# A hybrid decoder layer on one core: the operand tiles of the up and down projections are moved to other bytes of SBUF

## The chip, the cores and the metric

The kernel runs on one core of one Trainium2 chip. The metric is the device time of one execution in microseconds (us). A profile of one execution lies beside the times; its span runs from the first to the last instruction of the program, and it is a little shorter than the execution's own time.

In what follows a *byte* of a tile is its address inside one SBUF partition: all 128 partitions hold a tile at the same byte. A matmul instruction has two SBUF operands. The *stationary* one (128 x 128) is loaded into the array by a weight load ahead of it; the *moving* one (128 rows of N columns) streams through. One moving *row* here means the N contiguous float32 values that one matmul reads in each partition, so a row of 256 is 1024 bytes.

## The reference

One layer of a hybrid decoder: an RMS norm, a combined input projection, differential attention beside a gated linear recurrence (HGRN2), an output projection with a residual, and a feed-forward part with a causal convolution of width 3. The change lies in the feed-forward part:

```python
D_MODEL = 1024; SEQ = 1024; D_FF = 2816; CONV_WIDTH = 3
def conv_ffn(a, w_up, conv_w, conv_b, w_down):
    u = a @ w_up
    u = lax.conv_general_dilated(u, conv_w[:, None, :], ...) + conv_b
    gate, up = jnp.split(u, 2, axis=-1)
    return (jax.nn.gelu(gate, approximate=True) * up) @ w_down
...
    a = rmsnorm(h, ln_ffn_pre[l])
    y = conv_ffn(a, w_ffn_up[l], ffn_conv_w[l], ffn_conv_b[l], w_ffn_down[l])
    h = h + rmsnorm(y, ln_ffn_post[l])
```

## The kernel before

**Precision.** Every float32 matrix product is made of three matmuls: each operand is split into a rounded high part and the rest (`split`, lines 146 to 151; `t_split`, lines 1222 to 1226), and high x high, high x low and low x high are summed in PSUM. The low parts are made by VectorE or GpSimd, the high parts by ScalarE.

**The up stage** multiplies the 1024 model columns by the 2 x 2816 columns of `w_up`. The sequence is worked on in two pieces, p = 0 and p = 1, and each product is a Strassen-like scheme of seven products, j = 0 to 6, on quarters of the operands. The moving operands are the split tiles `tt[p][j]`: four rows of high parts, then four rows of low parts, each row `WN[p]` long, 258 for p = 0 and 256 for p = 1. `t_tiles` (1215) allocates them; `t_split` fills them; `t_sums` (1233) makes those of j = 1, 2, 3, 5 from sums of quarters. The stationary operands are the split weights `uh`, `ul`, made two products ahead by `prep` (1107).

The first feature tile is done by `plain_unit` (1316) with eight plain products instead of seven; `t_sums` of both pieces run beside it. The other 21 feature tiles go through `unit` (1335), which both pieces step through in turn (loop at 1453): product j of p = 0, product j of p = 1, then j + 1. `mm` (1341) is one such product: twelve matmuls, called a *block* here:

```python
for k in range(4):
    s = slice(P * k, P * (k + 1))
    T.matmul(pt, hi[:, s], th[:, k], ...)   # line 1346
    T.matmul(pt, hi[:, s], tl[:, k], ...)   # line 1347
    T.matmul(pt, lo[:, s], th[:, k], ...)   # line 1348
```

TensorE's order is written out by hand (`manual_schedule`), so its instructions run in program order. Products 0 and 4 add into the PSUM tile `pa`, 1, 3 and 5 into `pb`, 2 and 6 into `pc`. Behind the last product of a feature tile `gated` (1309) does the convolution (`conv`, 1300), the gate and the store of the result to `gsc` in DRAM.

**The down stage** multiplies the gated tiles, read back from DRAM, by `w_down`, again in seven products (`ORDER`, 1403) of eleven steps each. `operands` (1423) loads and splits both sides of a step three steps ahead (`LOOK`). Here the gated tile `gh`, `gl` is the stationary side (four slices of 128 columns) and the weight tile `wh`, `wl` is the moving side, 512 columns. One step is twelve matmuls (`mms`, 1499, lines 1504 to 1506), 77 steps in all.

**The out stage** ahead of the up stage (`out_part`, 997, lines 1002, 1004, 1006) also has moving rows of 512, `wo`, against stationary slices of the tiles `mp`. The change doesn't touch it, but the prediction reads some of its rows.

**Where the tiles lie.** Pools are stacked from both ends of a partition: those on the left grow upward, those on the right downward, and in a pool the tags follow one another in the order in which they are first asked for. This is the allocation of the program before, with the remainder by 512, of the rows that the matmuls read:

| tile | role | pool | base byte | base mod 512 | row pitch |
|---|---|---|---|---|---|
| t0_6, t0_5 | moving, N = 258 | mix (`X1`, `X2`) | 5856, 14112 | 224, 288 | 1032 |
| t1_6 | moving, N = 256 | mix (`X0`) | 22368 | 352 | 1032 |
| t1_0, t1_4, t1_5 | moving, N = 256 | tsplit | 51424, 59616, 67808 | 224 | 1024 |
| t0_1, t0_2, t0_3 | moving, N = 258 | tsplit | 76000, 84256, 92512 | 224, 288, 352 | 1032 |
| t1_1, t1_2, t1_3 | moving, N = 256 | tsplit2 | 100768, 108960, 117152 | 416 | 1024 |
| t0_4, t0_0 | moving, N = 258 | early | 163680, 171936 | 352, 416 | 1032 |
| uh, ul | stationary, up | weights, sums | several | 480 | 512 (slice) |
| gh, gl | stationary, down | down | 136896 and on | 192 | 512 (slice) |
| wh, wl | moving, N = 512, down | weights | 212960 and on | 480 | one row |

t0_7 and t1_7, which only `plain_unit` reads, lie where t0_5 and t1_5 lie later. Of the out stage, the first two steps read moving rows at byte class 480 (mod 512) with stationary slices of the first block at class 224 and of the second at class 288.

Of the kernel before, what the change touches and what calls it, by code (L numbers as in the profile page):

```python
# [9 lines left out]
F32 = mybir.dt.float32  # L10
F32R = mybir.dt.float32r
# [6 lines left out]
P = 128  # L18
# [13 lines left out]
WN = [258, 256]  # L32
# [53 lines left out]
def layer_kernel(ctx: ExitStack, tc: tile.TileContext, x, meta, table, lbl, gpre, gpost, win,  # L86
# [7 lines left out]
    def pool(name, bufs, side="left", space=None):  # L94
        kw = {"side": side} if space is None else {"space": space}
        cm = tc.tile_pool(name=name, bufs=bufs, reuse_waits="tile", **kw)
        return cm, cm.__enter__()

    def close(*cms):
        for cm in cms:  # L100
            cm.__exit__(None, None, None)
# [63 lines left out]
    mx_cm, mxp = pool("mix", 1)  # L165
# [1046 lines left out]

    tt = [[None] * 8 for _ in range(2)]

    def t_tiles(p, j, where, tag):
        if len(tag) == 1:
            both = where.tile([P, 8, WN[p]], F32R, tag=tag[0], name=f"t{p}_{j}")
            return both[:, 0:4], both[:, 4:8]
        both = where.tile([P, 8, int(tag[1])], F32R, tag=tag[0], name=f"t{p}_{j}")
        return both[:, 0:4, : WN[p]], both[:, 4:8, : WN[p]]  # L1220

    def t_split(p, j, src, where, *tag):
        hi, lo = t_tiles(p, j, where, tag)
        A.copy(hi, src)
        V.tensor_tensor(lo, src, hi.bitcast(F32), op=ALU.subtract)
        tt[p][j] = (hi, lo)

    def quarter(p, j):
        n = WN[p]
        a, c = {0: (0, 0), 7: (0, n), 4: (4, 0), 6: (4, n)}[j]  # L1230
        return at2[p][:, a:a + 4, c:c + n]

    def t_sums(p, where, last):
        b11, b12, b21, b22 = (quarter(p, j) for j in (0, 7, 4, 6))
        V.tensor_tensor(b11, b12, b11, op=ALU.subtract)
        V.tensor_tensor(b12, b22, b12, op=ALU.subtract)
        V.tensor_tensor(b22, b22, b11, op=ALU.subtract)
        t_split(p, 1, b22, where, f"t{p}_1")
        t_split(p, 2, b11, where, f"t{p}_2")
        t_split(p, 3, b12, where, f"t{p}_3")  # L1240
        V.tensor_tensor(b21, b21, b22, op=ALU.subtract)
        t_split(p, 5, b21, *last)

# [47 lines left out]

    xu_cm, xup = pool("xu", 2)
    t_cm, tp = pool("tsplit", 1)

    marks = {}

# [85 lines left out]
        next(p0)  # L1382
    trans(8)
    t_split(1, 7, quarter(1, 7), tp, "t1_5")
    t_split(1, 6, quarter(1, 6), mxp, "X0", WN[0])
    t_sums(0, tp, (mxp, "X2", WN[0]))
    close(a_cms.pop())
    t2_cm, t2p = pool("tsplit2", 1)
    p1 = plain_unit(1, ps_b)
    for j in range(4):  # L1390
        prep(7 + j)
        next(p1)
    t_sums(1, t2p, (tp, "t1_5"))
    close(a_cms.pop(), b_cm)
    v_cm, cv = pool("conv", 2, "right")
    dn_cm, dn = pool("down", 4, "right")
    next(p0)
    for j in range(4, 7):
# [257 lines left out]
```

## Time and profile before

| | us |
|---|---|
| median of 3 runs (lowest, highest) | 1313.61 (1312.26, 1313.94) |
| the profiled execution's own time | 1313.97 |
| its span | 1312.2 |
| up stage, first to last matmul of lines 1346 to 1348 | 663.5 to 1085.3, 3528 matmuls |
| down stage, first to last matmul of lines 1504 to 1506 | 1085.4 to 1302.7, 924 matmuls |

The mean granted clock of TensorE was 0.996 over the span.

How to read it. PE is TensorE's matmul side and PEld its weight loads, which overlap the matmuls; DVE is VectorE, ACT ScalarE, POOL GpSimd. A matmul row of the timeline has its start, its duration and its form ("128x256" is a moving operand of 256 columns). Matmuls are pipelined: a row lasts some 0.28 us, but the next one starts much earlier, so the time that a matmul costs is the step from its start to the start of the next. The program's names stand without their numbers (`t` for t1_2, `uh` for a split weight), so a block is told by its place: each feature tile runs the fourteen blocks (j, p) = (0,0), (0,1), (1,0), (1,1), ... (6,1) in this order.

### The profile page before, as it was taken

To read this page: it belongs to the slowest core of one execution; us is meant where nothing else is said; L and a number is where in the kernel's file an instruction comes from. 1 tells how busy PE (TensorE), PEld (TensorE's weight loads), DVE (VectorE), ACT (ScalarE), POOL (GpSimd) and SP (SyncE) were. 2 spreads that over 40 slices of the span, in tenths; PEclk is the share of its full clock that TensorE was granted. 3 is DMA by queue.
4 is the path that set the end of the run, shared out by engine and by line. 5 is a ranking of instruction groups with operands and counts; after the bars stand their busy time and mean duration, and the time that the engine had idled before them with its cause. 6 is when DMAs were issued, how large, how long until landed. Compare 5 with 4: busy or idle time off the path is not lost.

```text
span 1312.2 us, 26128 instructions
## 1 busy us (share of the span) xinstructions
PE 1283.2 (98%) x10172; PEld 1184.9 (90%) x10172; DVE 884.6 (67%) x1487; ACT 694.8 (53%) x1635; POOL 484.7 (37%) x384
## 2 busy tenths in 40 slices
PE   8999999999999999899999999999999999999997
PEld 7899999999999998677999999999999997888875
DVE  6564646465645574548897877778778767697586
ACT  8475466546644765247754544544544445464453
POOL 5231423242323310335066576666666631010121
PEclk9999999999999999999999999999999999999999
DMA  6244655173644534586322222222222138865263
GB/s 211 93 94 92 118 120 114 54 143 84 120 122 79 121 109 143 173 267 236 130 65 82 89 73 81 77 86 81 73 76 95 57 102 275 314 200 161 88 209 121
DMA packets 116322, 165.00 MB, mean 126 GB/s; under 512 B 10035, under 2 KB 57427, under 8 KB 116198
## 3 DMA queue, kind: packets, MB, share of 16 engines
q1 hardware_dynamic: 92966, 151.79, 35.6%
q0 software_dynamic: 23232, 11.54, 7.5%
q8 instruction: 80, 1.31, 0.4%
q14 instruction: 44, 0.36, 0.1%
HBM read 134.19 MB, written 52.17 MB: 142 GB/s over the span
## 4 chain that ended last, share of the span: by engine, by line
PE 83%; DVE 6%; ACT 4%; DMA 3%; issue 2%; POOL 2%; SPq 0%; DVEq 0%; ACTq 0%; POOLq 0%
PE pd L1505 5%; PE pd L1506 5%; PE pd L1504 5%; PE pb L1346 4%; PE pb L1347 4%; PE pb L1348 4%; PE pa L1346 3%; PE pa L1348 3%; PE pa L1347 3%; PE pc L1346 3%; PE pc L1347 3%; PE pc L1348 3%; PE pa L723 3%; PE pi_hf L232 1%; PE pi_dk L236 1%
## 5 line engine op out<-in xcount | busy, mean ns | idle before, releaser
L1346 PE MATMUL pb<-t,uh 128*128 128x258 f32 x504 | 142.3, 282 | 2.5 <-DVE u L53 2.5
L1347 PE MATMUL pb<-t,uh 128*128 128x258 f32 x504 | 141.7, 281 | 0.0
L1348 PE MATMUL pb<-t,ul 128*128 128x258 f32 x504 | 141.5, 281 | 0.0
L1505 PE MATMUL pd<-wl,gh 128*128 128x512 f32 x308 | 122.0, 396 | 1.2 <-DVE wl L53 1.1
L1504 PE MATMUL pd<-wh,gh 128*128 128x512 f32 x308 | 121.7, 395 | 0.0
L1506 PE MATMUL pd<-wh,gl 128*128 128x512 f32 x308 | 121.6, 395 | 0.0
L53 DVE SCALAR_TENSOR_TENSOR c<-uu,cwt,c 128x514 f32<-128x514 f32 (+1 forms) x88 | 97.2, 1105 | 19.6 <-ACT c L53 18.9
L53 POOL TENSOR_TENSOR c<-c,c 128x514 f32<-128x514 f32 (+1 forms) x44 | 63.6, 1445 | 122.7 <-ACT c L53 120.6
L1346 PEld LDWEIGHTS pb<-t,uh 128*128 128x128 f32 x504 | 95.4, 189 | 3.0 <-DVE u L53 2.9
L1347 PEld LDWEIGHTS pb<-t,uh 128*128 128x128 f32 x504 | 95.5, 189 | 0.0
L1346 PE MATMUL pa<-t,uh 128*128 128x258 f32 (+1 forms) x336 | 95.2, 283 | 0.0
L1348 PEld LDWEIGHTS pb<-t,ul 128*128 128x128 f32 x504 | 95.2, 189 | 0.0
L1348 PE MATMUL pa<-t,ul 128*128 128x258 f32 (+1 forms) x336 | 95.1, 283 | 0.0
L1347 PE MATMUL pa<-t,uh 128*128 128x258 f32 (+1 forms) x336 | 94.8, 282 | 0.0
L1346 PE MATMUL pc<-t,uh 128*128 128x258 f32 (+1 forms) x336 | 94.4, 281 | 0.0
L1347 PE MATMUL pc<-t,uh 128*128 128x258 f32 (+1 forms) x336 | 94.0, 280 | 0.0
L1348 PE MATMUL pc<-t,ul 128*128 128x258 f32 (+1 forms) x336 | 93.7, 279 | 0.0
L53 DVE SCALAR_TENSOR_TENSOR c<-ug,cwt,c 128x514 f32<-128x514 f32 (+1 forms) x88 | 88.3, 1004 | 1.4 <-ACT c L53 0.6
L53 POOL TENSOR_TENSOR ul<-ws,uh 128x512 fp32r<-128x512 f32 x42 | 60.7, 1444 | 35.4 <-ACT uh L53 35.4
L1505 PEld LDWEIGHTS pd<-wl,gh 128*128 128x128 f32 x308 | 57.7, 187 | 16.5 <-DVE wl L53 2.5
L53 ACT CAST uh<-ra 128x512 fp32r<-128x512 f32 x67 | 41.0, 617 | 59.6 <-PE pb L1347 41.0
L53 DVE TENSOR_TENSOR ul<-ra,uh 128x512 fp32r<-128x512 f32 x42 | 38.6, 920 | 48.1 <-ACT uh L53 48.1
(374 smaller groups left out, 4178.3 us busy)
## 6 DMA issues: line engine op xcount, KB each, us to landing
ra<-in_wup_dram SPq DMA_DIRECT2D x88, 256.0 KB, 2.7
mp<-msc SPq DMA_DIRECT2D x23, 512.0 KB, 5.2
tsc<-in_wdown_dram SPq DMA_DIRECT2D x44, 256.0 KB, 4.9
wi<-tsc SPq DMA_DIRECT2D x44, 256.0 KB, 3.1
gi<-gsc SPq DMA_DIRECT2D x33, 256.0 KB, 4.3
wi<-in_wdown_dram SPq DMA_DIRECT2D x33, 256.0 KB, 5.3
gsc<-c SPq DMA_DIRECT2D x22, 257.0 KB, 2.1
tsc<-in_wdown_dram POOLq DMA_DIRECT2D x22, 256.0 KB, 7.2
```

Source lines behind the costliest of these rows:

```text
L53: ins = call(*args, **kw)
L232: T.matmul(pt, hi[:, s], ahi[:, k, t0:t1], start=(k == 0), stop=False)
L236: T.matmul(pt, lo[:, s], ahi[:, k, t0:t1], start=False, stop=(k == KD - 1))
L723: T.matmul(po[:, :P], w_, vn[:, j], start=(j == 0), stop=(j == i))
L1346: T.matmul(pt, hi[:, s], th[:, k], start=(first and k == 0), stop=False, skip_group_check=True)
L1347: T.matmul(pt, hi[:, s], tl[:, k], start=False, stop=False, skip_group_check=True)
L1348: T.matmul(pt, lo[:, s], th[:, k], start=False, stop=(k == 3), skip_group_check=True)
L1504: T.matmul(py, gh[:, s], wh, start=(k == 0 and pr not in (3, 7)), stop=False, skip_group_check=True)
L1505: T.matmul(py, gh[:, s], wl, start=False, stop=False, skip_group_check=True)
L1506: T.matmul(py, gl[:, s], wh, start=False, stop=(k == NH - 1), skip_group_check=True)
```

## The change

Tiles get other bytes. `t_tiles` allocates flat tiles and cuts the eight rows out of them with a pitch and an offset that are given with the tag; the tiles t0_1, t0_2, t0_3 get a pitch of 288 values and t0_3 an offset of 6; t1_6 gets its own length 256 as pitch and an offset of 16 values. Two tiles that nothing reads or writes are allocated ahead of others: `gap` (48 values) as the first of the pool tsplit, `gap2` (56 values) as the first of the pool of the convolution, which lies above the pool of the down stage's operands. No instruction is added or removed, and no shape of an operand changes.

```diff
+    ROW = 288
+
     def t_tiles(p, j, where, tag):
-        if len(tag) == 1:
-            both = where.tile([P, 8, WN[p]], F32R, tag=tag[0], name=f"t{p}_{j}")
-            return both[:, 0:4], both[:, 4:8]
-        both = where.tile([P, 8, int(tag[1])], F32R, tag=tag[0], name=f"t{p}_{j}")
-        return both[:, 0:4, : WN[p]], both[:, 4:8, : WN[p]]
+        tag, w, off = (tag + (WN[p], 0)[len(tag) - 1:])[:3]
+        n = 8 * w if w > WN[p] else 8 * w + off
+        flat = where.tile([P, n], F32R, tag=tag, name=f"t{p}_{j}")
+        if w > WN[p]:
+            both = flat.rearrange("p (a c) -> p a c", a=8)[:, :, off:off + WN[p]]
+        else:
+            both = flat[:, off:].rearrange("p (a c) -> p a c", a=8)
+        return both[:, 0:4], both[:, 4:8]
...
-        t_split(p, 1, b22, where, f"t{p}_1")
-        t_split(p, 2, b11, where, f"t{p}_2")
-        t_split(p, 3, b12, where, f"t{p}_3")
+        for j, b in ((1, b22), (2, b11), (3, b12)):
+            t_split(p, j, b, where, f"t{p}_{j}", *(() if p else (ROW, 6 if j == 3 else 0)))
...
     t_cm, tp = pool("tsplit", 1)
+    tp.tile([P, 48], F32, tag="gap", name="gap")
...
-    t_split(1, 6, quarter(1, 6), mxp, "X0", WN[0])
+    t_split(1, 6, quarter(1, 6), mxp, "X0", WN[1], 16)
...
     v_cm, cv = pool("conv", 2, "right")
+    cv.tile([P, 56], F32, tag="gap2", name="gap2", bufs=1)
     dn_cm, dn = pool("down", 4, "right")
```

## The prediction

> **What bounds the kernel now.** I read the page first, then the stages by windows, then the timeline of TensorE, block by block.
>
> ```profile
> span 1312.2 us, 26128 instructions
> PE 1283.2 (98%) x10172; PEld 1184.9 (90%) x10172; DVE 884.6 (67%) x1487; ACT 694.8 (53%) x1635; POOL 484.7 (37%) x384
> PE 83%; DVE 6%; ACT 4%; DMA 3%; issue 2%; POOL 2%; SPq 0%; DVEq 0%; ACTq 0%; POOLq 0%
> L1346 PE MATMUL pb<-t,uh 128*128 128x258 f32 x504 | 142.3, 282 | 2.5 <-DVE u L53 2.5
> L1505 PE MATMUL pd<-wl,gh 128*128 128x512 f32 x308 | 122.0, 396 | 1.2 <-DVE wl L53 1.1
> ```
>
> TensorE carries 83% of the chain that ended last. The windows (us, then busy us of each engine, clock, DMA share, GB/s) show how full it is where the change works:
>
> ```profile
> 663.40:1085.50 422.10, 419.62 (x3532) 419.07 (x3531) 321.59 (x466) 205.01 (x363) 263.54 (x182) 1.00 0.25 83
> 1085.50:1312.20 226.70, 216.44 (x925) 172.61 (x923) 167.22 (x243) 109.45 (x219) 26.78 (x17) 0.99 0.58 194
> 663.40:703.60 40.20, 37.72 (x314) 37.17 (x313) 34.48 (x44) 20.77 (x37) 31.51 (x19) 1.00 0.24 80
> 703.60:743.80 40.20, 40.20 (x341) 40.20 (x341) 30.23 (x45) 19.54 (x36) 25.75 (x19) 1.00 0.24 79
> 1085.00:1125.00 40.00, 38.90 (x169) 31.05 (x168) 30.10 (x44) 20.95 (x36) 3.30 (x2) 1.00 0.87 299
> 1125.00:1205.00 80.00, 80.00 (x344) 64.22 (x343) 64.57 (x101) 39.13 (x75) 6.42 (x4) 1.00 0.63 206
> ```
>
> From 703.6 on TensorE is never idle in the up stage, at the full granted clock, and VectorE, the next engine, is at 30.23 of 40.20 (75%). In the down stage VectorE is at 64.57 of 80 (81%). So a nanosecond off each matmul is a nanosecond off the end, as long as VectorE keeps up. The three rows in which it doesn't (start, duration, and in brackets the idle time and who ended it):
>
> ```profile
> 673.28 0.39 PE L1346 MATMUL pb<-t,uh 128*128 128x258 f32 x1 [1.08 <-DVE u L53]
> 680.68 0.39 PE L1346 MATMUL pb<-t,uh 128*128 128x258 f32 x1 [1.40 <-DVE u L53]
> 1092.48 0.50 PE L1505 MATMUL pd<-wl,gh 128*128 128x512 f32 x1 [1.10 <-DVE wl L53]
> ```
>
> Now one feature tile, the first matmul of each block and of the tile after it. A block is twelve matmuls; the step between two rows is its time.
>
> ```profile
> 726.58 0.28 PE L1346 MATMUL pa<-t,uh 128*128 128x258 f32 x1
> ...
> 728.02 0.28 PE L1346 MATMUL pa<-t,uh 128*128 128x256 f32 x1
> ...
> 729.46 0.28 PE L1346 MATMUL pb<-t,uh 128*128 128x258 f32 x1
> ...
> 730.90 0.28 PE L1346 MATMUL pb<-t,uh 128*128 128x256 f32 x1
> ...
> 732.31 0.28 PE L1346 MATMUL pc<-t,uh 128*128 128x258 f32 x1
> ...
> 733.73 0.28 PE L1346 MATMUL pc<-t,uh 128*128 128x256 f32 x1
> ...
> 735.09 0.29 PE L1346 MATMUL pb<-t,uh 128*128 128x258 f32 x1
> ...
> 736.54 0.28 PE L1346 MATMUL pb<-t,uh 128*128 128x256 f32 x1
> ...
> 737.92 0.29 PE L1346 MATMUL pa<-t,uh 128*128 128x258 f32 x1
> ...
> 739.37 0.28 PE L1346 MATMUL pa<-t,uh 128*128 128x256 f32 x1
> ...
> 740.80 0.28 PE L1346 MATMUL pb<-t,uh 128*128 128x258 f32 x1
> ...
> 742.22 0.28 PE L1346 MATMUL pb<-t,uh 128*128 128x256 f32 x1
> ...
> 743.65 0.28 PE L1346 MATMUL pc<-t,uh 128*128 128x258 f32 x1
> ...
> 745.09 0.28 PE L1346 MATMUL pc<-t,uh 128*128 128x256 f32 x1
> ...
> 746.51 0.28 PE L1346 MATMUL pa<-t,uh 128*128 128x258 f32 x1
> ```
>
> The steps, with the base bytes mod 512 of the table of tiles:
>
> - N = 256: t1_0 1.44 (byte 224), t1_1 1.41 (416), t1_2 1.36 (416), t1_3 1.38 (416), t1_4 1.43 (224), t1_5 1.43 (224), t1_6 1.42 (352, pitch 1032). Sum 9.87 us.
> - N = 258: t0_0 1.44, t0_1 1.44, t0_2 1.42, t0_3 1.45, t0_4 1.45, t0_5 1.42, t0_6 1.44.
>
> All N = 256 blocks do the same work with the same kind of weights, yet they take from 1.36 (113.3 ns a matmul) to 1.44 (120 ns). The three at class 224 are the slow ones and the three at class 416 the fast ones. But t1_1 and t1_2 have the same class and differ by 0.05: the byte is not all of it, something of what ran before a block stays in its pace.
>
> **The change part by part.** Nothing is computed anew; only bytes move.
>
> *The gap in tsplit, the offset of t1_6.* 48 values are 192 bytes, so t1_0, t1_4, t1_5 go to 51616, 59808, 68000: class 416. The pool grows by 192 bytes and by 3 x (9216 - 8256) bytes for the longer pitch, so tsplit2 goes up by 3072 = 6 x 512 and t1_1 to t1_3 stay at class 416. t1_6 starts 64 bytes later with a pitch of 1024: 22432, class 416. All seven N = 256 blocks then read every row at class 416. Bounds: at best all run like t1_2, 7 x 1.36 = 9.52, 0.35 us less for each of 21 feature tiles, 7.4 us; at worst all stick at the pace of t1_0, 7 x 1.44 = 10.08, 4.4 us lost. The mean of the three that are there today is 1.383, which makes 9.68 and 4.0 us. Two of these three (t1_2, t1_3) are near 1.37; I take 1.37, since the blocks of p = 0 that run between lose some of their odd bytes too: 9.59, 0.28 x 21 = **5.9 us**.
>
> *The pitch of 288.* t0_1, t0_2, t0_3 go to 76192, 85408 and 94624 + 24 = 94648. Rows are 1152 bytes apart, so their classes are 416, 32, 160, 288 (t0_3: 440, 56, 184, 312), the same for high and low parts, where today each row begins 8 bytes further than the one before and the low ones 32 bytes off. No block of 258 columns with such rows is in the trace. Today the three take 1.44 + 1.42 + 1.45 = 4.31. From above, the pace of t1_2 for 258 columns, 12 x 258 x 0.1133 / 256 = 1.37 each, saves 0.20 x 21 = 4.2 us; from below, all at 1.45 loses 0.8 us. They become as regular as the p = 1 tiles at 416, whose mean of 1.383 is a little above the best, so I take 1.40: 0.11 x 21 = **2.3 us**.
>
> *The four p = 0 tiles left alone* and the 48 p = 0 matmuls of the first feature tile: nothing (plus or minus 0.01 us a block by what runs before them, 0.8 us for all). The p = 1 half of the first feature tile, 96 matmuls at t1_0's pace, gains at most 96 x 6.7 ns = 0.6 us, of which I take 0.2: VectorE makes the sums then. The first feature tile behind it waits twice for VectorE (1.08 and 1.40 us); what TensorE gains there, about 0.4 us, it waits longer: minus 0.4. ScalarE and VectorE write the moved tiles once, with as many elements. Up stage: 5.9 + 2.3 + 0.2 - 0.4 = **8.0 us**.
>
> *The second gap.* 56 values are 224 bytes; the down pool hangs below, so `gh` and `gl` go from class 192 to 480, the class of the moving `wh` and `wl`, which stay. A run of the down stage today, 114 matmuls apart:
>
> ```profile
> 1179.87 0.40 PE L1504 MATMUL pd<-wh,gh 128*128 128x512 f32 x1
> ...
> 1206.47 0.39 PE L1504 MATMUL pd<-wh,gh 128*128 128x512 f32 x1
> ```
>
> 26.60 / 114 = 233.3 ns. Other stationary bytes under the same moving class stand in the out stage, six matmuls from each row to the next, first with slices at class 224, then at class 288:
>
> ```profile
> 510.40 0.39 PE L1002 MATMUL py<-woh,mp 128*128 128x512 f32 x1
> ...
> 511.76 0.40 PE L1002 MATMUL py<-woh,mp 128*128 128x512 f32 x1
> ...
> 513.16 0.39 PE L1002 MATMUL py<-woh,mp 128*128 128x512 f32 x1
> ```
>
> 1.36 / 6 = 226.7 ns, then 1.40 / 6 = 233.3. The first six have stationary and moving rows 256 bytes apart in class, equal mod 256, as the down stage will have them. Best: 6.7 ns x 924 = 6.2 us. Worst: t1_0 too has both sides equal mod 256 (224 and 480) and runs at 120 / 113.3 of the best; a down stage slowed alike runs at 240, 6.2 us lost. I take three quarters of the good end, **4.6 us**, as the good row has the same shape, and six matmuls behind another stage are a short proof. The wait of 1.10 us at 1092 swallows 24 matmuls' gain, 0.2 us, inside that quarter.
>
> [...]
>
> Sum: 8.0 + 4.6 = 12.6 us off 1313.97, the profiled execution's own time (1.8 above its span), which is 0.4 above the median; off the median, 1313.6 - 12.6 = **1301.0**.
>
> **The rivals.**
>
> *The stationary byte does nothing; only the up stage gains*: 1313.6 - 8.0 = 1305.6. For it: runs of six are short. Against: 1.36 and 1.40 in a row.
>
> *Bytes are inert; the pace of a block comes from its place*, from which PSUM tile it adds to or what runs beside it. Then nothing moves: 1313.6. For it: t1_1 and t1_2 differ at one class. Against: t1_0, t1_4 and t1_5, in three places and two PSUM tiles, are all slow and all at 224. [...]
>
> *Equal classes collide.* In the down stage weight load and moving row walk through the same byte class at once, as in t1_0: 240 ns, 6.2 us lost. It ends above the time before once the up stage brings less than 6.2, say when the N = 258 rows gain nothing and the N = 256 blocks keep their mean of today's three less some entries, about 2 us: 1313.6 + 6.2 - 2 = 1317.8. For it: t1_0 has equal classes and the slowest pace. Against: the six at 226.7.
>
> *VectorE becomes the bound.* Up: 30.23 per 40.20; 2% faster blocks make it 77%. It can't take the gain except where it already does.
>
> **How the numbers follow.** Forecast (both stages gain, in whatever shares) 0.50; up alone 0.26; nothing 0.09; collision 0.15. A measurement of this kernel can't tell less than 0.2% (2.6 us) from no change. Up alone is faster. Of the collision, a third still ends faster or level by the up stage. Faster 0.79, same 0.09, slower 0.12. Range: the best of all terms is 7.4 + 4.2 + 0.6 + 6.2 = 18.4, 1295.2, and 0.8 for the tiles left alone makes 1294.4; upward the range takes in no change, 1314: 1294 to 1314, leaving out the collision. The forecast's own range is 1294 to 1305.
>
> **What would show it.** Right: in one feature tile, the seven N = 256 blocks at 1.36 to 1.38 and the three with pitch 288 at 1.40 or less; 226 to 229 ns in the down stage; still no wait behind 703 us; the spans before 663 us unchanged. Wrong: N = 256 blocks at 1.41 or more in spite of class 416 (the entry decides, not the byte); 233 in the down stage (the stationary byte is inert) or 240 (collision); or new waits for VectorE that take what the blocks gain.

## The result and the profile after

| | before | changed |
|---|---|---|
| median of 6 runs each (lowest, highest) | 1313.78 (1312.26, 1316.96) | 1307.59 (1306.24, 1308.24) |
| span of the profiled execution | 1312.2 | 1305.7 |
| start of the span to the up stage's first matmul | 663.53 | 663.01 |
| up stage, first to last matmul | 421.74 | 420.47 |
| down stage, first to last matmul | 217.34 | 212.53 |
| behind it | 9.44 | 9.58 |

The ratio is 0.9947, with a 95% interval of 0.9933 to 0.9960. The change is faster, by half of what was forecast. The down stage gave 4.8 us, where 4.6 was forecast; the up stage gave 1.3 instead of 8.0.

The page of the changed kernel (busy times, the shares of the chain that ended last, two groups; the code's lines stand five further down in the up stage, 1351 to 1353, and six in the down stage, 1510 to 1512):

```profile
PE 1274.0 (98%) x10172; PEld 1181.6 (90%) x10172; DVE 885.2 (68%) x1487; ACT 693.8 (53%) x1635; POOL 484.7 (37%) x384
...
PE 81%; DVE 7%; ACT 4%; DMA 3%; POOL 2%; issue 2%; SPq 0%; DVEq 0%; POOLq 0%; ACTq 0%
...
L1351 PE MATMUL pb<-t,uh 128*128 128x258 f32 x504 | 142.4, 283 | 2.8 <-DVE u L53 2.7
...
L1511 PE MATMUL pd<-wl,gh 128*128 128x512 f32 x308 | 120.3, 391 | 2.1 <-DVE wl L53 2.0
```

TensorE's share of the chain fell from 83% to 81%, VectorE's rose from 6% to 7%, and the waits for it in the down stage from 1.1 to 2.0 us. The windows of both stages and of the same 80 us of the down stage that was shown of before:

```profile
663.00:1083.50 420.50, 417.74 (x3530) 416.71 (x3529) 322.60 (x466) 203.91 (x362) 263.22 (x182) 1.00 0.25 83
1083.50:1305.70 222.20, 210.95 (x927) 173.02 (x925) 167.37 (x243) 110.00 (x220) 26.75 (x17) 0.99 0.59 199
...
1125.00:1205.00 80.00, 79.96 (x353) 65.91 (x352) 66.24 (x104) 39.53 (x75) 6.43 (x4) 1.00 0.66 214
```

353 matmuls fit into 80 us where 344 did. Three waits for VectorE stand in the down stage now, where there was one of 1.10 us that the idle column showed (timeline of TensorE, idle time in brackets), and 114 undisturbed matmuls take 1193.04 - 1167.19 = 25.85 us, 226.7 ns each:

```profile
1090.78 0.50 PE L1511 MATMUL pd<-wl,gh 128*128 128x512 f32 x1 [1.34 <-DVE wl L53]
...
1167.19 0.39 PE L1510 MATMUL pd<-wh,gh 128*128 128x512 f32 x1
...
1193.04 0.39 PE L1510 MATMUL pd<-wh,gh 128*128 128x512 f32 x1
...
1244.12 0.50 PE L1511 MATMUL pd<-wl,gh 128*128 128x512 f32 x1 [0.38 <-DVE wl L53]
...
1274.64 0.50 PE L1511 MATMUL pd<-wl,gh 128*128 128x512 f32 x1 [0.30 <-DVE wl L53]
```

The feature tile whose block starts were shown of before, now in the changed kernel, with the first row of the feature tile ahead of it:

```profile
706.16 0.28 PE L1351 MATMUL pa<-t,uh 128*128 128x258 f32 x1
...
725.99 0.28 PE L1351 MATMUL pa<-t,uh 128*128 128x258 f32 x1
...
727.42 0.28 PE L1351 MATMUL pa<-t,uh 128*128 128x256 f32 x1
...
728.84 0.28 PE L1351 MATMUL pb<-t,uh 128*128 128x258 f32 x1
...
730.28 0.28 PE L1351 MATMUL pb<-t,uh 128*128 128x256 f32 x1
...
731.65 0.28 PE L1351 MATMUL pc<-t,uh 128*128 128x258 f32 x1
...
733.08 0.28 PE L1351 MATMUL pc<-t,uh 128*128 128x256 f32 x1
...
734.50 0.39 PE L1351 MATMUL pb<-t,uh 128*128 128x258 f32 x1
734.73 0.29 PE L1352 MATMUL pb<-t,uh 128*128 128x258 f32 x1
...
736.07 0.29 PE L1351 MATMUL pb<-t,uh 128*128 128x256 f32 x1
...
737.45 0.29 PE L1351 MATMUL pa<-t,uh 128*128 128x258 f32 x1
...
745.91 0.28 PE L1351 MATMUL pa<-t,uh 128*128 128x258 f32 x1
```

Three things are to be seen. The tile from 706.16 to 725.99 takes 19.83 us (19.93 before), the next one, to 745.91, takes 19.92. In the second one the first matmul of t0_3, at 734.50, lasts 0.39 us instead of 0.28, and the next starts 0.23 us later instead of 0.12. And t1_2 takes 734.50 - 733.08 = 1.42 us, though its byte class is still 416; before it took 1.36.

The row with 0.39 us shows no idle time in brackets, because the rows ahead of it, 0.28 us long, reach past its start. But it has the duration of the rows that wait for VectorE (673.28 and 680.68 of before), and it is found in every second feature tile, from the second to the twentieth. `pb` is read by the add `u2 = pb + x1` of product 1 before product 3 may add into it. VectorE at that place, first in the kernel before, then in the changed one (start and duration; two adds, for p = 0 and p = 1, are one row):

```profile
733.89 0.68 DVE L53 TENSOR_TENSOR ul<-ws,uh 128x512 fp32r<-128x512 f32 x1
734.49 0.75 DVE L53 TENSOR_TENSOR u<-pb,x 128x258 f32<-128x258 f32 x2
```

```profile
733.43 0.68 DVE L53 TENSOR_TENSOR ul<-ws,uh 128x512 fp32r<-128x512 f32 x1
734.03 0.74 DVE L53 TENSOR_TENSOR u<-pb,x 128x258 f32<-128x258 f32 x2
```

Before, the first add began 734.49 - 726.58 = 7.91 us behind the feature tile's first matmul, and t0_3 began at 735.09, 8.51 us behind it. Now the add begins at 8.04 us and ends some 0.4 us later, and t0_3 still begins at 8.51. VectorE has no idle time ahead of these rows: it works through the convolution of the feature tile before and two low parts `ul`, the second of them (product 1's weights for the next feature tile; `prep` works seven products ahead, not two) right ahead of the adds.

The rest is told by the steps of the blocks. This table holds, for each block and kernel, the median over the 21 feature tiles of its time divided by its twelve matmuls, in ns, worked out from the starts in each trace. The kernels are those of the experiments below.

| block | before | pitch alone (3rd) | p = 1 at 416 (2nd) | changed | p = 1 at 416, VectorE relieved (9th) |
|---|---|---|---|---|---|
| t1_0 | 119.8 | 119.8 | 118.0 | 118.0 | 118.0 |
| t1_1 | 117.9 | 117.8 | 113.3 | 113.8 | 113.3 |
| t1_2 | 113.3 | 113.8 | 130.8 with the wait | 118.2 | 113.3 |
| t1_3 | 114.7 | 114.8 | 114.7 | 117.8 | 114.7 |
| t1_4 | 119.2 | 119.2 | 114.7 | 113.7 | 114.7 |
| t1_5 | 119.3 | 119.3 | 113.3 | 113.3 | 113.3 |
| t1_6 | 118.6 | 118.6 | 114.3 | 114.3 | 114.3 |
| t0_1 | 120.1 | 120.1 | 118.2 | 120.6 | 118.2 |
| t0_2 | 118.2 | 120.6 | 119.5 | 119.6 | 119.5 |
| t0_3 | 120.9 | 119.2 | 128.2 with the wait | 127.8 with the wait | 120.9 |
| t0_5 | 118.4 | 118.4 | 119.5 | 119.5 | 119.5 |
| t0_6 | 120.1 | 120.1 | 122.3 | 122.3 | 122.3 |

t0_0 and t0_4 stay within 0.6 ns everywhere. A median hides one thing: in the changed kernel t1_3 takes 117.8 ns in the feature tiles without the wait, and 113.2 to 114.9 in seven of the nine from the fourth to the twentieth that have it. So the short wait, some 0.1 us, went with another pace of a block behind it in those seven.

### The profile page after: what moved, and what is told of

The parts are those of the page before. It is cut to its first block, busy times and chain, and to the rows that moved or that the text cites. A ratio compares the mean times of both kernels' runs of the same rounds, so it can differ in the third digit from the quotient of the medians.

```text
span 1305.7 us, 26127 instructions
## 1 busy us (share of the span) xinstructions
PE 1274.0 (98%) x10172; PEld 1181.6 (90%) x10172; DVE 885.2 (68%) x1487; ACT 693.8 (53%) x1635; POOL 484.7 (37%) x384
## 4 chain that ended last, share of the span: by engine, by line
PE 81%; DVE 7%; ACT 4%; DMA 3%; POOL 2%; issue 2%; SPq 0%; DVEq 0%; POOLq 0%; ACTq 0%
PE pd L1511 5%; PE pd L1512 5%; PE pd L1510 5%; PE pb L1351 4%; PE pb L1352 4%; PE pb L1353 4%; PE pa L1351 3%; PE pa L1352 3%; PE pa L1353 3%; PE pc L1353 3%; PE pc L1352 3%; PE pc L1351 3%; PE pa L723 3%; DMA wor<-in_wout_dram 1%; PE pi_hf L232 1%
## 5 line engine op out<-in xcount | busy, mean ns | idle before, releaser
L1510 PE MATMUL pd<-wh,gh 128*128 128x512 f32 x308 | 119.8, 389 | 0.0
L53 POOL TENSOR_TENSOR c<-c,c 128x514 f32<-128x514 f32 (+1 forms) x44 | 63.5, 1444 | 122.6 <-ACT c L53 119.2
```

The costliest lines, as they stand in the source:

```text
L53: ins = call(*args, **kw)
L1510: T.matmul(py, gh[:, s], wh, start=(k == 0 and pr not in (3, 7)), stop=False, skip_group_check=True)
```

## The experiments

Eleven kernels ran. The first four have one profiled execution and one time each, beside 1311.83 us of the kernel before; their verdicts rest on the steps of their traces. The part ahead of the up stage, which the edits leave all but untouched, took from 661.5 to 665.8 us in the profiled executions, so a stage's own length says more than a time.

**First: the second gap alone.**

```diff
 v_cm, cv = pool("conv", 2, "right")
+cv.tile([P, 56], F32, tag="gap2", name="gap2", bufs=1)
```

against the kernel before.

> The kernel before with the second gap alone (56 values, stationary gh and gl from class 192 to 480); all up-stage tiles at their old bytes. Theory (the pace follows the bytes of both operands): the down stage, first to last matmul, takes 212.5 us as in the changed kernel (217.3 before) at 226.7 ns a matmul, the up stage 421.7 as before, the execution 4.8 less than the kernel before. Rival (the down stage is faster because the up stage hands over in another state): the down stage stays at 217.3 and 233.3 ns.

Measured: 1309.29 us; up stage 421.72, all block steps as before; down stage 212.44. The same 80 us in its trace:

```profile
1125.00:1205.00 80.00, 79.95 (x353) 65.89 (x352) 66.20 (x104) 40.29 (x77) 6.45 (x4) 1.00 0.65 219
```

The whole gain of the down stage is this one gap. Of the tiles that matmuls read, only the stationary `gh` and `gl` moved (and with them the raw tiles that some of them are split from), so here the stationary side's byte set the pace of matmuls whose moving rows lie where they lay: 353 of them in the 80 us instead of 344, 80 / 353 = 226.6 ns each instead of 232.6.

**Second: the p = 1 tiles at 416 without the pitch, and another class for gh.**

```diff
-    ROW = 288
+    ROWS = {}
...
-            t_split(p, j, b, where, f"t{p}_{j}", *(() if p else (ROW, 6 if j == 3 else 0)))
+            t_split(p, j, b, where, f"t{p}_{j}", *(() if p else ROWS.get(j, ())))
...
 t_split(1, 7, quarter(1, 7), tp, "t1_5")
+tp.tile([P, 80], F32, tag="gapb", name="gapb")
...
-cv.tile([P, 56], F32, tag="gap2", name="gap2", bufs=1)
+cv.tile([P, 16], F32, tag="gap2", name="gap2", bufs=1)
```

against the changed kernel. t0_1, t0_2 and t0_3 keep the pitch and the classes of before; `gh` and `gl` go to class 128.

> All seven p = 1 tiles at class 416, all p = 0 tiles at the classes they had before (pitch 1032); the second gap is 16 values, which puts gh and gl at class 128. If the byte class of a block alone sets its pace: t1_0, t1_4, t1_5, t1_6 go to 113 to 114 ns, every p = 0 block keeps its old time (119.9, 120.0, 118.0, 120.7, 120.8, 118.3, 120.0 ns), t1_1 stays at 117.8; the up stage is 5 us shorter than 421.7. If a block hands a state on to the next: p = 0 blocks behind the moved ones change by 1 to 3 ns although no byte of theirs moved, and the up stage gains 2 to 4 us. Down stage: if only equal classes help, class 128 under 480 stays at 233.3 ns; if any step away from class 192 helps, 226.7.

Measured: 1311.59 us; up stage 420.51, down stage 218.16. The windows row of 1125 to 1205 us is back at 344 matmuls: class 128 brings nothing. In the up stage the seven p = 1 blocks run at 118.0 and 113.3 to 114.7 ns, and still it is no shorter than the changed kernel's. Three feature tile starts, and the place between the second and the third:

```profile
704.79 0.28 PE L1351 MATMUL pa<-t,uh 128*128 128x258 f32 x1
...
724.50 0.28 PE L1351 MATMUL pa<-t,uh 128*128 128x258 f32 x1
...
732.80 0.28 PE L1353 MATMUL pc<-t,ul 128*128 128x256 f32 x1
733.13 0.39 PE L1351 MATMUL pb<-t,uh 128*128 128x258 f32 x1
733.36 0.28 PE L1352 MATMUL pb<-t,uh 128*128 128x258 f32 x1
...
744.54 0.28 PE L1351 MATMUL pa<-t,uh 128*128 128x258 f32 x1
```

One feature tile takes 19.71 us, the next 20.04. In the longer one the last matmul of t1_2 starts at 732.80 and t0_3 comes 0.33 us later. VectorE there:

```profile
732.07 0.68 DVE L53 TENSOR_TENSOR ul<-ws,uh 128x512 fp32r<-128x512 f32 x1
732.67 0.74 DVE L53 TENSOR_TENSOR u<-pb,x 128x258 f32<-128x258 f32 x2
```

The first add begins 8.17 us behind the feature tile's start; product 3 could have begun at 8.42, as in the tile before, and begins at 8.63. The first six blocks end 0.09 us earlier than in the changed kernel (8.42 against 8.51), and the wait costs more, 20.04 - 19.71 = 0.33 us a feature tile against 19.92 - 19.83 = 0.09. Of the two expectations for the blocks the second came true: t0_1, t0_2, t0_5 and t0_6 changed by 1.1 to 2.3 ns though their classes didn't. Neither had the waits, and the up stage gained 1.2 us instead of 2 to 4.

**Third: the pitch alone.**

```diff
+ROWS = {1: (288, 0), 2: (288, 0), 3: (288, 6)}
...
 t_split(1, 7, quarter(1, 7), tp, "t1_5")
+tp.tile([P, 48], F32, tag="gapb", name="gapb")
...
+cv.tile([P, 40], F32, tag="gap2", name="gap2", bufs=1)
```

against the kernel before; `ROWS` holds pitch and offset of t0_1, t0_2, t0_3, and `gh` and `gl` go to class 32.

> Only t0_1, t0_2, t0_3 moved as in the change (pitch 288, offset 6 of t0_3, classes 416 and 440); all p = 1 tiles at their old classes; the second gap is 40 values, which puts gh and gl at class 32. Theory (the new pitch does not help, it costs): t0_1, t0_2, t0_3 together take 10 to 60 ns more a feature tile than before, t1_1 runs at 113.7 and t1_2 at 117.8 as in the changed kernel, though neither moved, and the up stage is level or up to 1.5 us longer than 421.7. Rival (the pitch gains, the p = 1 moves cost): the up stage is 2 us or more shorter. Down stage: 233.3 ns if only class 480 helps, 226.7 otherwise.

Measured: 1314.23 us; up stage 422.04 (421.74 before), down stage 218.01, 345 matmuls in the 80 us. t0_2 loses 2.4 ns a matmul, t0_3 gains 1.8, t0_1 and all p = 1 blocks stay within 0.5. The pitch alone is worth nothing. (Here as in the change the three tiles also start at class 416 or 440, where they stood at 224, 288 and 352; pitch and start were not moved apart, and "the pitch" means both.) The expectation had t1_1 at 113.7 and t1_2 at 117.8. That they didn't change here shows that what moved them in the changed kernel needs the moved p = 1 tiles too.

**Fourth: the p = 1 tiles at the class of the weights.**

```diff
 t_cm, tp = pool("tsplit", 1)
+tp.tile([P, 64], F32, tag="gap", name="gap")
...
 t_split(1, 7, quarter(1, 7), tp, "t1_5")
+tp.tile([P, 64], F32, tag="gapb", name="gapb")
...
 t2_cm, t2p = pool("tsplit2", 1)
+t2p.tile([P, 16], F32, tag="gapt", name="gapt")
...
+cv.tile([P, 56], F32, tag="gap2", name="gap2", bufs=1)
```

against the kernel before. t1_0 to t1_5 go to class 480, that of `uh` and `ul`; the tile t1_6 stays.

> Six p = 1 tiles (all but t1_6, which stays as before) at class 480, the class of their stationary uh and ul, with the p = 0 tiles at their old classes; the second gap as in the change. If equal classes are what helped the down stage, the six run at 113.3 ns or less and the up stage is 4 us or more shorter than 421.7. If equal classes collide at N = 256, as t1_0 at 224 under 480 (equal mod 256) did, the six run at 120 ns and the up stage is 2 us longer. Down stage 212.5 us in both.

Measured: 1311.19 us; up stage 424.78, 3.0 longer than before; t1_0 to t1_5 all at 118.7 to 119.8 ns; down stage 212.69. So at N = 256 equal classes of stationary and moving rows were the slow case here (t1_0 at 224, equal mod 256, was slow before too, at 119.8), and at N = 512 in the down stage they were the fast one (353 matmuls in the 80 us, where the kernel before had 344). One rule "equal is good" or "equal collides" for both shapes is wrong. Every third feature tile from the fifth on has a wait at t0_3 here too (20.11 to 20.15 us instead of 20.08), though TensorE is slower than before: how late VectorE came here depended on more than TensorE's pace.

**Fifth: VectorE relieved in the changed kernel.** The low part of product 1's weights is made by GpSimd, against the changed kernel:

```diff
-        split(hi, lo, src, G if j % 2 == 0 and j else V)
+        split(hi, lo, src, G if j % 2 == 0 and j or j == 1 else V)
```

> The changed kernel with one thing moved: the low part of product 1's weights (one subtraction a feature tile, which stands on VectorE right ahead of the two adds u2 that product 3 waits for) is made by GpSimd. Theory: in every second feature tile the adds end 8.46 us behind the tile's first matmul and hold up product 3; without the 0.6 us ahead of them they end near 7.9, the 224 to 227 ns at the first matmul of t0_3 go back to about 120, and the up stage loses those waits, ten times some 0.11 us, and what the first feature tile's two waits for VectorE give back: 420.47 to 418 or 419 us, the time to 1305.5. Rival, the long first matmul is TensorE's own way of entering this tile: the up stage stays at 420.5 and the time at 1307.6.

Measured: 1308.88 us (5 runs, 0.9965 of before, 0.9952 to 0.9978); up stage 420.51. Feature tile starts, and t0_3 in the second of them:

```profile
705.41 0.28 PE L1351 MATMUL pa<-t,uh 128*128 128x258 f32 x1
...
725.24 0.28 PE L1351 MATMUL pa<-t,uh 128*128 128x258 f32 x1
...
733.75 0.28 PE L1351 MATMUL pb<-t,uh 128*128 128x258 f32 x1
...
745.07 0.28 PE L1351 MATMUL pa<-t,uh 128*128 128x258 f32 x1
```

Every feature tile from the second to the last now takes 19.83 us, and t0_3 starts with the usual 0.28. The wait was VectorE's. The expected microsecond is gone all the same, since the first feature tile through `unit` takes 24.09 us instead of 23.05: its two waits for VectorE grew. The sum is the rival's 420.5, but not for the rival's reason.

```profile
671.84 0.39 PE L1351 MATMUL pb<-t,uh 128*128 128x258 f32 x1 [1.70 <-DVE u L53]
679.85 0.39 PE L1351 MATMUL pb<-t,uh 128*128 128x258 f32 x1 [2.08 <-DVE u L53]
```

In the changed kernel they are 1.28 and 1.43. My expectation had them shrink. VectorE and GpSimd ahead of the first wait, in the changed kernel and then here:

```profile
671.21 0.74 DVE L53 SCALAR_TENSOR_TENSOR c<-uu,cwt,c 128x514 f32<-128x514 f32 x1
672.10 1.60 POOL L53 TENSOR_TENSOR c<-c,c 128x514 f32<-128x514 f32 x1 [1.36 <-DVE c L53]
```

```profile
669.18 1.73 POOL L53 TENSOR_TENSOR ul<-ws,uh 128x512 fp32r<-128x512 f32 x1
669.69 1.76 DVE L53 SCALAR_TENSOR_TENSOR c<-uu,cwt,c 128x514 f32<-128x514 f32 x1
```

The last pass of the convolution took 0.74 us while GpSimd stood idle (1.36 us, to 672.10), and takes 1.76 beside the low part that GpSimd makes now. That is 1.02 us more, less the 0.60 that VectorE no longer spends on the low part: 0.42, by which the first wait grew (1.28 to 1.70).

**Sixth: the same relief in the kernel before**, the same edit as in the fifth.

> The same move of one low part to GpSimd in the kernel before, as a control: what VectorE's relief is worth where no block has become faster. Theory: product 3 never waits behind 703 us there, so only the two waits of the first feature tile (1.08 and 1.40 us) can shrink: up stage 421.7 to between 419.8 and 421.7, time 1311.8 to 1313.8. Rival, VectorE's queue slows every feature tile: all block steps fall and the up stage with them, to 418 or less.

Measured: 1314.74 us (10 runs, 1.0012, 1.0001 to 1.0023); up stage 424.06. From the third feature tile on all take 19.93 us, as without the relief: there VectorE was never late. The second takes 19.93 instead of 20.14, so before it already held a wait that the idle column didn't show. The first takes 25.51 us instead of 22.98, with waits of 1.51 and 2.02 us, so the expectation missed here too, and by more than in the fifth; the section on the hardware says why.

**Seventh: only the later p = 1 tiles.**

```diff
 t_split(1, 0, quarter(1, 0), tp, "t1_0")
+tp.tile([P, 48], F32, tag="gap", name="gap")
 t_split(1, 4, quarter(1, 4), tp, "t1_4")
...
 t_split(1, 7, quarter(1, 7), tp, "t1_5")
-t_split(1, 6, quarter(1, 6), mxp, "X0", WN[0])
+tp.tile([P, 80], F32, tag="gapb", name="gapb")
+t_split(1, 6, quarter(1, 6), mxp, "X0", WN[1], 16)
...
+cv.tile([P, 56], F32, tag="gap2", name="gap2", bufs=1)
```

against the kernel before; t0_1 to t0_3 keep their classes.

> Second gap as in the change; of the p = 1 tiles only t1_4, t1_5 and t1_6 go to class 416, t1_0 stays at 224 and all p = 0 tiles keep the bytes and the pitch of before. The three stand behind the adds that VectorE is late with. Theory: t1_4, t1_5, t1_6 at 114.7, 113.3 and 114.3 ns (119.2, 119.3, 118.6 before) bring 0.18 us a feature tile, t0_5 and t0_6 behind them give back 0.04 (119.5 and 122.3), the first six blocks stay as before, no new wait at t0_3: up stage 421.7 - 21 x 0.14 = 418.8 us, time about 1306.4, a little under the change with half of its moves. Rival, what these blocks gain makes VectorE late all the same, since its chain starts with them: waits at t0_3 in every second feature tile, up stage 420.5 or more, time 1308 or more.

Measured: 1307.94 us (5 runs, 0.9959, 0.9945 to 0.9973); up stage 420.72. The rival came out. t1_4, t1_5 and t1_6 run at 114.7, 113.3 and 114.3, t0_5 and t0_6 at 119.5 and 122.3, and the undisturbed feature tiles take 19.79 us, the 0.14 less that was expected. But every second one takes 19.95 with a wait at t0_3, and gains nothing. My reading is that what these last blocks gain reaches the next feature tile as VectorE's delay: the convolution starts with them, and its eight passes took VectorE 8.3 to 8.4 us a feature tile both in the kernel before and in the changed one (second to nineteenth through `unit`). For this kernel itself that isn't shown.

**Eighth: p = 1 at 416, no pitch, the second gap, and the relief.**

```diff
-cv.tile([P, 16], F32, tag="gap2", name="gap2", bufs=1)
+cv.tile([P, 56], F32, tag="gap2", name="gap2", bufs=1)
...
-split(hi, lo, src, G if j % 2 == 0 and j else V)
+split(hi, lo, src, G if j % 2 == 0 and j or j == 1 else V)
```

against the second kernel.

> All p = 1 tiles at class 416, no pitch of 288 and no moved p = 0 byte (as in the second experiment), the second gap at its full 56 values, and product 1's low part on GpSimd. Theory: the second experiment's 24 waits for VectorE (6.7 us in the up stage) go, the blocks keep their paces: up stage 420.5 - 6 = 414.5 us, down stage 212.5, time near 1301.5. Rival, the waits are TensorE's own or VectorE is late for its other work (the four passes of conv): up stage 419 to 420.5, time 1306 to 1307.5.

Measured: 1306.69 us (4 runs, 0.9947, 0.9932 to 0.9962); up stage 418.07, down stage 212.91. All feature tiles from the second on take 19.71 us: the waits are gone, as the theory has it. The size was off: of the second experiment's 6.7 us of waits 3.3 are in the first feature tile, which the edit doesn't shorten but lengthens to 24.05. The up stage ends between the theory (414.5) and the rival (419 or more), and the time is in the rival's range.

**Ninth: the same with the relief only from the third feature tile on.**

```diff
-split(hi, lo, src, G if j % 2 == 0 and j or j == 1 else V)
+split(hi, lo, src, G if j % 2 == 0 and j or j == 1 and q > 21 else V)
```

> All p = 1 tiles at class 416, p = 0 as before, the second gap at 56 values, and product 1's low part on GpSimd only from the third feature tile on, so that the first keeps its order. Theory: every feature tile from the third on takes 19.71 us, the first 23.05 instead of 24.05: up stage 417.1 us, down stage 212.7; with 661.5 to 663.5 us ahead of the up stage the time is 1303 to 1305. Rival, the first tile's extra microsecond has nothing to do with the low part: up stage 418.1, time 1304 to 1306.

Measured: 1305.08 us (6 runs, 1303.36 to 1305.86; 0.9929, 0.9914 to 0.9943); the window of its up stage, feature tile starts, and VectorE in the tile between the last two:

```profile
662.00:1079.10 417.10, 414.33 (x3530) 413.94 (x3529) 305.86 (x447) 204.00 (x362) 300.04 (x201) 1.00 0.25 83
```

```profile
704.76 0.28 PE L1351 MATMUL pa<-t,uh 128*128 128x258 f32 x1
...
724.47 0.28 PE L1351 MATMUL pa<-t,uh 128*128 128x258 f32 x1
...
732.88 0.29 PE L1351 MATMUL pb<-t,uh 128*128 128x258 f32 x1
...
744.17 0.28 PE L1351 MATMUL pa<-t,uh 128*128 128x258 f32 x1
```

```profile
729.59 2.45 DVE L53 SCALAR_TENSOR_TENSOR c<-ug,cwt,c 128x510 f32<-128x510 f32 x2
731.96 0.74 DVE L53 TENSOR_TENSOR u<-pb,x 128x258 f32<-128x258 f32 x2
```

The adds follow the convolution directly and begin 7.49 us behind the start, t0_3 at 8.41. The first feature tile takes 23.05 us, the others 19.71: both as expected, and the up stage's 417.07 is the 417.1 of the theory. The time, 0.08 us above the theory's 1303 to 1305, is in the rival's range too; the stage's length, 418.1 by the rival, decides between them. VectorE gave up 16.7 us of work in the stage (322.60 to 305.86), and POOL's rose by 36.8 (263.22 to 300.04).

**Tenth: a pitch that keeps rows equal mod 256, and a class equal mod 256 in the down stage.**

```diff
+ROWS = {1: (320, 0)}
...
-tp.tile([P, 80], F32, tag="gapb", name="gapb")
...
 for j, b in ((1, b22), (2, b11), (3, b12)):
+    if (p, j) == (0, 2):
+        where.tile([P, 96], F32, tag="gapb", name="gapb")
...
-cv.tile([P, 56], F32, tag="gap2", name="gap2", bufs=1)
+cv.tile([P, 120], F32, tag="gap2", name="gap2", bufs=1)
```

against the ninth kernel. The rows of t0_1 lie at classes 416 and 160 in turn, the moved gap keeps t0_2 and t0_3 at their classes, and `gh` and `gl` go to class 224.

> The ninth kernel with two things more. t0_1 gets a row pitch of 320 values (1280 bytes): its rows lie at classes 416 and 160 in turn, all equal mod 256, while its columns stay 258. And the second gap is 120 values, so that gh and gl lie at class 224, equal to that of wh and wl (480) mod 256 only. If equal rows are what makes a block fast, t0_1 falls from 118.2 to about 114 ns and the up stage by 1 us, to 416.1; rival, 258 columns have a pace of their own whatever the rows: t0_1 stays between 118 and 120.6. If the down stage's pace needs equal classes mod 512, its step goes to 233 ns and the stage to 218 us; if mod 256 is enough, it stays at 226.7 and 212.7.

Measured: 1305.74 us (6 runs, 0.9934, 0.9919 to 0.9949); up stage 418.14, down stage 213.09. The start of t0_1, of t1_1 behind it, and the 80 us of the down stage:

```profile
749.01 0.28 PE L1353 MATMUL pb<-t,uh 128*128 128x258 f32 x1
...
750.46 0.28 PE L1353 MATMUL pb<-t,uh 128*128 128x256 f32 x1
```

```profile
1125.00:1205.00 80.00, 79.95 (x353) 65.87 (x352) 66.94 (x104) 40.24 (x77) 6.45 (x4) 1.00 0.65 217
```

t0_1 takes 1.45 us, 120.8 ns a matmul (118.2 in the ninth), and t1_1 behind it 115.3 instead of 113.3. Rows equal mod 256 didn't make this block of 258 columns fast. In the down stage equal mod 256 was enough: 353 matmuls, as at class 480.

**Eleventh: the changed kernel again**, beside the ninth and tenth.

> The changed kernel itself, beside the two above on one chip, for a direct comparison: 1307.6, up stage 420.5 us. Theory: the ninth kernel is 3 us faster than this one in the up stage and equal elsewhere. Rival: the differences between executions ahead of the up stage (661.5 to 665.8 us so far) cover it.

Measured: 1307.01 us (6 runs, 1305.87 to 1308.67; 0.9947, 0.9932 to 0.9961), up stage 420.45, down stage 212.96. The ninth kernel's six runs all lie below these six, by a hair, though the intervals against the kernel before overlap; its up stage is 3.4 us shorter. It has the lowest median of the kernels tried; the tenth, 0.66 us above it, isn't told apart from it by the times.

## Why the prediction was right or wrong

**Direction and range were right, the forecast was 6.6 us too low**, and the whole of that is in the up stage.

**The p = 1 blocks at class 416 (5.9 us): right by itself.** Without the pitch and without waits (ninth) their sum is 9.62 us a feature tile, where 9.59 was taken: 9.87 - 9.62 = 0.25 us, 5.3 us over 21. The sum is right, the picture of seven equal blocks is not: t1_0 keeps 118.0 ns (1.42 us) at class 416, which the prediction had named as a sign against the byte. The p = 0 blocks behind give back 0.03 us (10.06 to 10.09), which the term "four p = 0 tiles left alone, nothing" had within its 0.8 us: t0_5 and t0_6 became slower by 1.1 and 2.3 ns with their bytes unmoved, in every kernel in which t1_4 to t1_6 went to 416. A feature tile goes from 19.93 to 19.71 us.

**The pitch of 288 (2.3 us): the step that failed.** "They become as regular as the p = 1 tiles at 416" is what the runs deny. The three rows are at 1.44, 1.43 and 1.45 us, not at 1.40, and with the pitch of 320, its rows equal mod 256, t0_1 wasn't faster either (120.8 ns against 118.2). It costs more than it fails to gain: the fifth and the eighth kernel both have p = 1 at 416 and the relief, and only the fifth has the pitch; their feature tiles take 19.83 and 19.71 us (the start bytes that go with the pitch are part of this difference). Over the 20 feature tiles behind the first the pitch takes back 2.4 us of the 4.5 that the p = 1 tiles bring. The larger part, 9.70 - 9.62 = 0.08 us of the 0.12, is lost in p = 1 blocks, t1_2 (117.8 against 113.3 ns) and t1_3 (117.8 against 114.7), whose own classes are the same in both. The prediction had seen that "something of what ran before a block stays in its pace" and priced it at 0.01 us a block for the tiles left alone; for t1_2 it was 0.05.

**VectorE ("It can't take the gain except where it already does"): wrong.** It took 0.7 us more of the changed kernel's up stage (what the feature tiles from the second on take above 19.83 us, 0.95, less the 0.21 us of waiting that the second tile had before), and it would have taken 3.4 us from the better layout of the second experiment: ten feature tiles at 20.04 instead of 19.71. The share of busy time that the prediction read, 75%, was an average over a feature tile. The first half of each second tile is full: there the adds of before end at 8.33 us and product 3 begins at 8.51. So a feature tile could lose less than 0.18 us before that wait began, and this was to be had from the timeline. The fifth, eighth and ninth kernels show it by the waits that went with one 0.6 us instruction, the seventh by waits that came though the first six blocks were hardly faster. "New waits for VectorE that take what the blocks gain" stood among the signs of being wrong, without a term in the sum.

**The first feature tiles (0.2 gained, 0.4 lost): right in sum.** The one through `plain_unit`, ahead of the up stage as measured here, has 192 matmuls, 96 of them p = 0 where the prediction counted 48; from the first to the last they take 24.41 us instead of 24.58. The one behind it takes 23.05 us instead of 22.98; its waits grew from 1.08 and 1.40 to 1.28 and 1.43, by 0.23.

These parts add up: 20 x 0.22 less 2.4, less 0.7, less 0.1 for the first through `unit` is 1.2 to 1.3 us, and 1.27 was measured.

**The second gap (4.6 us): right, with two errors that cancel.** The six matmuls of the out stage told the pace fully, not by three quarters: the mean step without waits fell from 233.3 to 226.8 ns, 6.0 us over 924. But new waits for `wl` and longer ones took 1.2 us back (steps above the pace: 2.0 us before, 3.2 now), where 0.2 was allowed. The first experiment, in which of the matmuls' operands only the stationary ones moved, has the term by itself: its down stage took 4.9 us less.

**The rivals.** "The stationary byte does nothing" and "bytes are inert" are refuted by the first and second experiments. "Equal classes collide" is wrong in the down stage and right in the up stage: the fourth experiment built it there, at 118.7 to 119.8 ns and 3.0 us lost. That weight load and moving row get in each other's way is not shown by that, only the pace. "VectorE becomes the bound" was dismissed; VectorE delays every second feature tile of the changed kernel.

**What stays open.** Which bytes are fast is measured, not explained: stationary at 480 or 224 against moving 480 at N = 512 was fast (353 matmuls in the 80 us), at 192, 128 and 32 it wasn't (344 or 345); moving 416 against stationary 480 at N = 256 was fast in the ninth kernel (113.3 to 114.7 ns), 480 (118.7 to 119.8) and 224 (119.2 to 119.8) were not, and t1_0 wasn't fast at 416 either (118.0). How a block hands its pace on was not separated from what its own bytes do. Which of start byte and pitch costs what in t0_1 to t0_3 wasn't tried.

## What to carry to other kernels

Where matmuls run back to back, the bytes of both operands were worth 3 to 5% of a step here (226.8 ns against 233.3 at N = 512, 113.3 against 119.3 for t1_5 at N = 256); measure the shape at hand, one tile at a time and in its place, since the class relation that was fast at one N was slow at another, and blocks whose bytes stay can become faster or slower with the blocks ahead of them (t0_1 from 120.1 to 118.2 ns in the ninth kernel, t0_6 from 120.1 to 122.3). Before counting on a gain of the busiest engine, read from the timeline of one period how early the next engine's result is there, not its share of busy time: here 75% busy hid a slack of less than 0.18 us. When an edit's gain is gone, look for a longer first instruction of the same kind at one place of every period: the waits in every second feature tile of the changed kernel stood in no idle column, only in a row of 0.39 us instead of 0.28. And when work goes from VectorE to GpSimd, look at what VectorE does beside it: in the fifth experiment a pass of the convolution took 1.76 us there instead of 0.74.

## What the runs showed of the hardware

In the kernel before each block's mean step is the same to 0.2 ns from the third to the twentieth feature tile: 113.3 to 119.8 ns at N = 256, at a granted clock of 1.00. Single steps inside these blocks last from 112 to 125 ns. At N = 512 in the down stage the mean without waits was 233.3 ns in the kernel before and 226.8 in the changed one.

A pass of the convolution over 128 x 514 values took VectorE 0.74 to 0.75 us in all 43 cases of the changed kernel's up stage in which GpSimd ran nothing beside it, and 1.41 to 1.79 us in the 21 in which GpSimd ran for at least nine tenths of it.

In the sixth experiment TensorE was idle for 2.02 us in the first feature tile. The row behind it, and the window behind that:

```profile
681.19 0.58 PE L1346 MATMUL pb<-t,uh 128*128 128x258 f32 x1 [2.02 <-DVE u L53]
```

```profile
681.20:684.70 3.50, 3.50 (x16) 3.50 (x17) 3.03 (x5) 0.00 (x0) 3.42 (x3) 0.51 0.17 65
```

The granted clock is 0.51 in this window; for about 3.4 us matmuls step by 215 ns instead of 120, and some 16 of them cost 1.5 us, more than half of what the first feature tile lost there. In the fifth, 2.08 us of idle time at the same place were followed by a clock of 1.00:

```profile
679.80:683.00 3.20, 3.15 (x27) 3.15 (x28) 2.99 (x5) 0.06 (x1) 3.12 (x3) 1.00 0.20 77
```

So the length of the idle time didn't decide alone: the slow stretch followed the shorter of the two. What did wasn't shown; no experiment changed the idle time by itself.
